# A down projection by seven products of quarters instead of eight, in a fused transformer layer on one core

## The chip, the cores and the metric

The kernel runs on one core of a Trainium2 chip. That core has five engines, each with a queue of its own that is worked off in order: TensorE (PE, products; PEld is its loading of the stationary operand), VectorE (DVE), ScalarE (ACT), GpSimd (POOL) and SyncE (SP, which here only issues transfers). They meet through semaphores. Products are written to banks of PSUM; all other tiles (named `block` in the profile) lie in SBUF. The metric is the device time of one execution in microseconds.

## The reference

One layer of a diffusion backbone on 512 latent tokens of width 1024, with 256 context tokens: attention and a state-space branch side by side, an output projection, and then a gated MLP. All in float32. What bears on the change is the end of it:

```python
def conv_glu(h, w_up, conv_w, conv_b, w_down):
    gate, val = jnp.split(h @ w_up, 2, axis=-1)
    gate = depthwise_conv(gate, conv_w, conv_b)
    return (jax.nn.gelu(gate, approximate=False) * val) @ w_down
...
        ffn_x = conv_glu(modulate(rms_norm(x, ffn_pre_norm[l]), mod_x[3], mod_x[4]),
                         w_up[l], ffn_conv_w[l], ffn_conv_b[l], w_down[l])
        x = x + mod_x[5] * rms_norm(ffn_x, ffn_post_norm[l])
```

The hidden width is 2816, so the down projection (`w_down`) is a product of 512 x 2816 by 2816 x 1024. Its rows are then normalised, multiplied by a row vector and added to x.

## The kernel before

Each float32 operand of a large product is split in two parts, `hi` (ScalarE copies the value into a shorter format, line 497) and `lo` (VectorE subtracts, line 498), and each product is done as three: hi x hi, hi x lo, lo x hi. So every operand costs a ScalarE copy and a VectorE subtraction, and every tile of a product three TensorE instructions.

The work runs in this order: modulation vectors and the input projections, the state-space branch beside the attention, the output projection (`natural_gemm`, products in line 1289), the up projection of the MLP (22 pairs of column blocks; products in line 751), the gating (`gated`, lines 1412 to 1423, one column block of 128 hidden units at a time, kept in `gT` with the hidden unit on the partition), and the down projection (lines 1469 to 1501). That last one runs over two halves of 512 output columns. For each half it takes the 22 hidden blocks in turn: the left operand (`gT[k]`, split once and kept for the second half), the right one (a 128x512 piece of the weights, loaded and split each time), and 4 tiles of 128 tokens x 3 products (line 1476). After the last blocks of a tile its squares are summed (line 1496), it is multiplied by the row `g2` (line 1497), and once both halves are there `last` normalises, adds and stores it (lines 1455 to 1467).

Three row vectors are computed as columns by `modfinish` (from line 1264). To become a row on all partitions a column is written to memory word by word (line 1276) and read back as one row for all 128 partitions (line 1278); both transfers are issued by GpSimd (`G`).

The order in which each engine does its work is set neither by the program text nor at run time. `plan` first traces the program, then places it by a list scheduler with prices for each kind of instruction, and at the same time gives each tile a place in the working memory of `UNITS` units of 1 KB per partition. What comes out is a fixed order on each engine. A tile whose place is taken waits until the former user has finished.

## Time and profile before

| what | value |
| --- | --- |
| median of 3 runs | 1001.02 us (999.69 to 1004.33) |
| span of the profiled execution, first to last instruction | 994.4 us |
| what lies around it, against the median of the runs | 6.6 us |
| last output-projection products end | about 619 us |
| last up-projection products end | 877.9 us |
| last down-projection products end | 986 us |

The profiled execution has no time of its own beside its span; the table sets the span against the median. The page of the profile lists the busy time of each engine, the chain of work that ended last, and groups of instructions by line with their mean duration. A line such as L498 is that of a helper, called from many places. "xN" is a count, "<-" after an idle time names what ended it. Shapes are partitions x elements.

### The profile page before, as it was taken

The page shows a single profiled execution, that of the slowest core. Times are in us where ns is not written, and L with a number is a line of the kernel's source. Part 1 is how long each engine was busy: PE and PEld are TensorE (multiplying, and loading weights), DVE is VectorE, ACT ScalarE, POOL GpSimd, SP SyncE. Part 2 cuts the span into 40 slices and gives each one's busy share as a digit, 9 for nine tenths or more (in the row PEclk, how much of TensorE's full clock was granted, in tenths as well). Part 3 has the DMA queues.
Part 4 walks back from the last instruction along what each step waited for, and adds up shares of the span by engine and source line. Part 5 has one row for each costly group of instructions (what it writes and reads, how often), then busy time and mean ns, then how long its engine had stood idle before and what let it go on. Part 6 is the DMA issues. An engine that isn't in the chain of part 4 may idle for free.

```text
span 994.4 us, 14412 instructions
## 1 busy us (share of the span) xinstructions
PE 971.8 (98%) x5224; PEld 825.9 (83%) x5224; DVE 700.9 (70%) x1304; ACT 501.4 (50%) x994; POOL 259.5 (26%) x223
## 2 busy tenths in 40 slices
PE   9999999999998999999999999999999999999996
PEld 8888888888876888888888888888888888888885
DVE  5999866988896989978789997952515442773406
ACT  4545337568566787687787324842314323452101
POOL 0001001765697886656541000000000000000000
PEclk7999999999998999999999999999999999999999
DMA  9922101012222242331566965431223221354422
GB/s 350 362 74 85 53 1 44 22 48 81 67 57 54 56 111 78 99 74 46 153 259 230 323 160 199 148 127 64 106 85 106 106 85 43 110 177 137 158 76 84
DMA packets 42214, 116.88 MB, mean 118 GB/s; under 512 B 5776, under 2 KB 8736, under 8 KB 42144
## 3 DMA queue, kind: packets, MB, share of 16 engines
q1 hardware_dynamic: 41440, 114.30, 34.8%
q0 software_dynamic: 528, 1.59, 0.5%
q8 instruction: 41, 0.67, 0.3%
q14 instruction: 29, 0.24, 0.1%
q10 hardware_dynamic: 176, 0.09, 0.0%
HBM read 96.02 MB, written 4.21 MB: 101 GB/s over the span
## 4 chain that ended last, share of the span: by engine, by line
PE 49%; DVE 6%; DMA 4%; issue 2%; ACT 1%; SPq 0%; POOL 0%; DVEq 0%; ACTq 0%; POOLq 0%
PE banks L751 26%; PE banks L1476 12%; PE banks L1175 4%; PE banks L1205 3%; PE banks L1193 2%; DVE block L498 2%; DMA block<-block 1%; DMA mod_rows<-mod 1%; DVE block L586 1%; PE banks L1109 1%; DMA block<-mod_rows 1%; ACT block L1179 1%; DVE smalls L1177 1%; DMA block<-in_wmod_dram 0%; DVE smalls L524 0%
## 5 line engine op out<-in xcount | busy, mean ns | idle before, releaser
L751 PE MATMUL banks<-block,block 128*128 128x512 f32 (+1 forms) x2132 | 448.3, 360 | 1.7 <-DVE block L1385 1.1
L751 PEld LDWEIGHTS banks<-block,block 128*128 128x128 f32 x2132 | 358.8, 188 | 62.5 <-issue 1.6
L498 DVE TENSOR_TENSOR block<-block,block 128x512 fp32r<-128x512 f32 (+5 forms) x252 | 227.0, 923 | 125.7 <-PE banks L751 47.8
L497 ACT ACTIVATE block<-block 128x512 fp32r<-128x512 f32 (+5 forms) x252 | 181.4, 743 | 207.8 <-PE banks L751 48.1
L1476 PE MATMUL banks<-block,block 128*128 128x512 f32 x496 | 116.6, 389 | 0.0
L1182 POOL TENSOR_TENSOR block<-block,smalls 128x768 f32<-128x768 f32 x64 | 97.3, 1527 | 60.7 <-DVE smalls L1181 38.4
L1476 PEld LDWEIGHTS banks<-block,block 128*128 128x128 f32 x496 | 93.0, 188 | 19.5
L1175 PE MATMUL banks<-block,block 128*128 128x512 f32 (+1 forms) x384 | 95.1, 357 | 1.4 <-DMA block<-block 0.7
L1276 POOL DMA_DIRECT2D mod_rows<-mod x3 | 2.9, 975 | 351.4 <-DVE mod L1272 351.4
L498 DVE TENSOR_TENSOR block<-banks,block 128x256 fp32r<-128x256 f32 (+1 forms) x156 | 83.2, 555 | 14.7 <-ACT block L497 12.9
L497 ACT ACTIVATE block<-banks 128x256 fp32r<-128x256 f32 (+1 forms) x156 | 73.0, 498 | 32.4 <-PE banks L1193 17.7
L1289 PE MATMUL banks<-block,block 128*128 128x512 f32 x384 | 88.6, 390 | 0.0
L1289 PEld LDWEIGHTS banks<-block,block 128*128 128x128 f32 x384 | 71.8, 188 | 14.5
L1193 PE MATMUL banks<-cst,block 128*128 128x128 f32 x384 | 66.9, 279 | 4.1 <-DVE block L498 3.7
L1205 PE MATMUL banks<-block,block 128*128 128x256 f32 x384 | 68.7, 299 | 0.8 <-DVE block L498 0.8
L1175 PEld LDWEIGHTS banks<-block,block 128*128 128x128 f32 x384 | 59.6, 190 | 10.2 <-ACT block L1179 2.7
L586 DVE SCALAR_TENSOR_TENSOR block<-block,block 128x1024 f32<-128x1024 f32 x52 | 62.6, 1219 | 4.1 <-DMA block<-in_wmod_dram 1.9
L1177 DVE TENSOR_REDUCE smalls<-banks 128x1 f32<-128x768 f32 x64 | 60.8, 950 | 6.6 <-PE banks L1175 5.9
L1179 ACT ACTIVATE block<-banks,smalls 128x768 f32<-128x768 f32 x64 | 57.7, 902 | 13.2 <-DVE smalls L1177 7.6
L786 DVE SCALAR_TENSOR_TENSOR block<-banks,cwh,block 128x510 f32<-128x510 f32 (+3 forms) x88 | 51.1, 620 | 14.4 <-ACT block L782 13.9
L1205 PEld LDWEIGHTS banks<-block,block 128*128 128x128 f32 x384 | 55.9, 191 | 5.3 <-DVE block L498 1.1
L1193 PEld LDWEIGHTS banks<-cst,block 128*128 128x128 f32 x384 | 47.7, 143 | 14.1 <-DVE block L498 3.9
(216 smaller groups left out, 1064.1 us busy)
## 6 DMA issues: line engine op xcount, KB each, us to landing
block<-in_wmod_dram SPq DMA_DIRECT2D x48, 512.0 KB, 6.9
block<-in_wup_dram SPq DMA_DIRECT2D x44, 512.0 KB, 3.8
block<-in_wdn_dram SPq DMA_DIRECT2D x44, 256.0 KB, 2.8
block<-block SPq DMA_DIRECT2D x32, 256.0 KB, 3.0
block<-in_wout_dram SPq DMA_DIRECT2D x16, 512.0 KB, 5.9
block<-block SPq DMA_DIRECT2D x56, 128.0 KB, 2.3
block<-in_wxbc_dram SPq DMA_DIRECT2D x12, 512.0 KB, 3.4
block<-in_wz_dram SPq DMA_DIRECT2D x16, 256.0 KB, 7.1
```

The costliest lines, as they stand in the source:

```text
L497: act(hi, src, AF.Copy)
L498: (lo_eng or V).tensor_tensor(out=lo, in0=src, in1=hi, op=ALU.subtract)
L586: V.scalar_tensor_tensor(out=junk, in0=wt, scalar=0.5, in1=vec, op0=ALU.mult, op1=ALU.mult, accum_out=acc)
L751: mm(po, lhsT=wf(k, pt[0]), rhs=xf(k, pt[1]), start=(k == 0 and pt == parts[0]), stop=(k == nk - 1 and pt == parts[-1]))
L1175: mm(sc[:, o : o + n], lhsT=q_[:, x_, qi * P : (qi + 1) * P], rhs=kk[:, y_, :], start=part == 0, stop=part == 2)
L1177: V.reduce_max(nm, sc[:, :T], axis=AX.X, negate=True)
L1179: act(pe, sc[:, :T], AF.Exp, bias=nm, scale=1.0, accum_out=sm_)
L1182: G.tensor_tensor(out=pe, in0=pe, in1=sm_.to_broadcast([P, T]), op=ALU.mult)
L1193: nc.tensor.transpose((tx if c < NX else tc_)[:, o : o + P], pe[:, s_ : s_ + P], ident)
L1205: mm(po[:, half * 256 : half * 256 + 256], lhsT=vst(c), rhs=rhs, start=(part == 0 and c == 0), stop=(part == 1 and c == NKT - 1))
L1289: mm(po[i][:, nh * 512 : nh * 512 + 512], lhsT=l[lp][:, i * P : (i + 1) * P], rhs=w[wp][:, nh * 512 : nh * 512 + 512], start=(k == 0 and l ...
L1476: mm(po[i], lhsT=l[lp][:, i * P : (i + 1) * P], rhs=w[wp], start=(k == 0 and lp == 0 and wp == 0), stop=(k == NF - 1 and lp == 1))
```

## The change

The down projection is now written as a product of 2 x 2 quarters: the tokens in two halves of 256, the hidden blocks in even and odd ones, the output columns in two halves of 512. Eight products of quarters would be needed in the plain way. Here seven are made, of sums and differences of quarters (the Winograd form of Strassen's scheme), and their results are combined.

- Left operands: for each pair of hidden blocks GpSimd computes four mixtures S1 to S4 of 128x256 (`mixed`, in `gated`). With A11, A12 and A22 from `gT` itself there are seven left operands; each is split when its sweep comes to it (so 7 x 11 splits of 128x256).
- Right operands: B11, B21, B22 are loaded; T1 to T4 are differences of loaded quarters, made on VectorE (`right_of`, line 1514 of the new kernel), T2 and T4 in the place of the former difference, T3 in the place of a loaded quarter. Each right operand is split too (7 x 11 splits of 128x512). 99 pieces of weights are loaded instead of 44.
- A `sweep` runs over the 11 pairs, with 2 tiles of 128 tokens x 3 products each (line 1521). Buffers are rotated: 6 for loaded pieces (`raws`), 8 for left operands (`ls`), 7 for right ones (`ws_`).
- The sweeps are, in the order of the program: S1 T1, S2 T2, A22 T4, S3 T3, A11 B11, S4 B22, A12 B21. The fourth, sixth and seventh go on adding to a bank of an earlier one. Copies of banks on ScalarE (line 1549) and sums on VectorE (lines 1555, 1572, 1574) give the four quarters of the output, and six of the eight multiplications by `g2` go to GpSimd (line 1482).
- `UNITS` is 212 instead of 200; a scratch area for transfers issued by GpSimd is made smaller in return.
- Both transfers of `modfinish` are issued by ScalarE.

```diff
-UNITS, EDGE, MARGIN = 200, 168, 2500
+UNITS, EDGE, MARGIN = 212, 168, 2500
...
         with nc.allow_non_contiguous_dma(reason="a column to a row"):
-            G.dma_start(out=scratch[n].rearrange("j p -> p j"), in_=ms)
+            nc.scalar.dma_start(out=scratch[n].rearrange("j p -> p j"), in_=ms)
         row = t4()
-        G.dma_start(out=row, in_=scratch[n : n + 1].rearrange("o j p -> o (j p)").to_broadcast([P, D]))
+        nc.scalar.dma_start(out=row, in_=scratch[n : n + 1].rearrange("o j p -> o (j p)").to_broadcast([P, D]))
...
         gT.append(cv)
+        if j % 2:
+            ga, gb = gT[-2:]
+            m = t4(P, 4, 256)
+            G.tensor_tensor(out=m[:, 0], in0=ga[:, late], in1=gb[:, late], op=ALU.add)
+            G.tensor_tensor(out=m[:, 1], in0=m[:, 0], in1=ga[:, early], op=ALU.subtract)
+            G.tensor_tensor(out=m[:, 2], in0=ga[:, early], in1=ga[:, late], op=ALU.subtract)
+            G.tensor_tensor(out=m[:, 3], in0=gb[:, early], in1=m[:, 1], op=ALU.subtract)
+            mixed.append([m[:, i] for i in range(4)])
...
+    def right_of(name, q):
+        if name[0] == "B":
+            return quarter(q, int(name[1]) - 1, int(name[2]) - 1)
+        x = quarter(q, *{"T1": (0, 1), "T2": (1, 1), "T3": (1, 1), "T4": (1, 0)}[name])
+        if name in ("T1", "T3"):
+            y = quarter(q, 0, 0 if name == "T1" else 1)
+            t = right[q] = t2() if name == "T1" else x
+        else:
+            t = y = right[q]
+        V.tensor_tensor(out=t, in0=x, in1=y, op=ALU.subtract)
+        return t
+
+    def sweep(po, lname, rname, first=False, done=None):
+
+        def products(i, q, l, w):
+            for n, (lp, wp) in enumerate(((0, 0), (0, 1), (1, 0))):
+                mm(po[i], lhsT=l[:, lp, i * P : (i + 1) * P], rhs=w[wp], start=first and q == 0 and n == 0,
+                   stop=q == PAIRS[-1] and n == 2, skip_group_check=not first)
 
         tail = []
...
+        for q in PAIRS:
+            l = nextof(ls)
+            split(l[:, 0, :], l[:, 1, :], left_of(lname, q))
+            ww = nextof(ws_)
+            w = ww[:, 0, :], ww[:, 1, :]
+            split(*w, right_of(rname, q))
+            if q in PAIRS[:-3]:
+                for i in range(2):
+                    products(i, q, l, w)
             else:
-                tail.append((k, w, lefts[k]))
+                tail.append((q, l, w))
...
+    sweep(W, "S1", "T1", first=True, done=kept(p5))
+    sweep(X, "S2", "T2", first=True, done=kept(p6))
+    sweep(Y, "A22", "T4", first=True)
...
+    sweep(X, "S3", "T3", done=after_p7)
...
+    sweep(Z, "A11", "B11", first=True, done=after_p1)
...
+    sweep(W, "S4", "B22", done=after_p3)
...
+    sweep(Z, "A12", "B21", done=after_p2)
...
-    nc = bacc.Bacc("TRN2", target_bir_lowering=False, num_devices=1)
+    nc = bacc.Bacc("TRN2", target_bir_lowering=False, num_devices=1, dynamic_dma_scratch_size=4096)
```

What the planner makes of it is seen in the order of each engine. A row names the line, the operation, the tile written, then the tiles read and the shape; `block_a_b` is the b-th tile, in a place of its own.

First VectorE in the down projection. Before, splits of weights follow one another:

```order
L498 TENSOR_TENSOR block_1213_7822<-block_1064_7171,block_1056_7057 128x512
L498 TENSOR_TENSOR block_1213_7822<-block_1064_7171,block_1203_7756 128x512
L498 TENSOR_TENSOR block_989_6546<-block_1092_7420,block_1056_7057 128x512
L498 TENSOR_TENSOR block_1062_7120<-block_1064_7171,block_1213_7822 128x512
L498 TENSOR_TENSOR block_971_6414<-block_1092_7420,block_1062_7120 128x512
```

In the changed kernel, in the stretch of the third and fourth sweep, there are three kinds (L1514 the differences of weights, L498 with 128x512 the right splits, with 128x256 the left ones):

```order
L1514 TENSOR_TENSOR block_1135_7543<-block_1018_6728,block_1135_7543 128x512
L1514 TENSOR_TENSOR block_1137_7570<-block_1018_6728,block_1137_7570 128x512
L498 TENSOR_TENSOR block_1126_7457<-block_1131_7489,block_1126_7457 128x512
L498 TENSOR_TENSOR block_1024_6737<-block_979_6453,block_1024_6737 128x256
L498 TENSOR_TENSOR block_865_5474<-block_1133_7516,block_865_5474 128x512
L498 TENSOR_TENSOR block_975_6398<-block_998_6588,block_975_6398 128x256
L1514 TENSOR_TENSOR block_1110_7456<-block_1110_7456 128x512
L1514 TENSOR_TENSOR block_1137_7570<-block_1108_7455,block_1137_7570 128x512
L1514 TENSOR_TENSOR block_1139_7585<-block_1108_7455,block_1139_7585 128x512
L498 TENSOR_TENSOR block_1076_7194<-block_1133_7516,block_1076_7194 128x512
```

Each step of the new sweeps has a left and a right split of its own, and in the first four a difference ahead of them, where before a step had at most one left and one right split.

Second, the transfers of the column-to-row step, in the output projection. Before, they stood on GpSimd, with nothing between them:

```order
L1276 DMA mod_rows<-mod 128x8x1
L1278 DMA block_769_5109<-mod_rows 128x1024
L1276 DMA mod_rows<-mod 128x8x1
L1278 DMA block_787_5183<-mod_rows 128x1024
L1357 TENSOR_TENSOR block_916_5755<-block_916_5755,block_769_5109 128x512
```

Now they stand on ScalarE, among copies of weights (L497) and sums of squares of the output projection's tiles (L1341):

```order
L1276 DMA mod_rows<-mod 128x8x1
L497 ACTIVATE block_883_5525<-block_624_4015 128x1024
L497 ACTIVATE block_888_5533<-block_733_4770 128x1024
L1278 DMA block_795_5180<-mod_rows 128x1024
L1276 DMA mod_rows<-mod 128x8x1
L1341 ACTIVATE block_771_5100,smalls<-banks 128x1024
L1341 ACTIVATE block_771_5100,smalls<-block_707_4588 128x1024
L497 ACTIVATE block_926_5810<-block_797_5183 128x1024
L1278 DMA block_786_5144<-mod_rows 128x1024
L497 ACTIVATE block_923_5805<-block_580_3726 128x1024
L497 ACTIVATE block_929_5863<-block_576_3712 128x1024
L1341 ACTIVATE block_703_4580,smalls<-banks 128x1024
```

A row transfer waits for the column transfer ahead of it to land, and what stands behind it waits with it.

Third, VectorE at the very end. Before, the last tile's chain (L524 and L528 are steps of the reciprocal root) runs straight to its own scale-and-add:

```order
L524 SCALAR_TENSOR_TENSOR smalls<-smalls 128x1
L528 SCALAR_TENSOR_TENSOR smalls<-smalls 128x1
L524 SCALAR_TENSOR_TENSOR smalls<-smalls 128x1
L528 SCALAR_TENSOR_TENSOR smalls<-smalls 128x1
L1466 SCALAR_TENSOR_TENSOR block_986_6541<-block_986_6541,smalls,block_968_6408 128x512 x2
```

Now (the same line is L1475) other tiles' scale-and-adds stand in that chain:

```order
L528 SCALAR_TENSOR_TENSOR smalls<-smalls 128x1 x2
L1475 SCALAR_TENSOR_TENSOR block_1104_7451<-block_1104_7451,smalls,block_1103_7446 128x512
L524 SCALAR_TENSOR_TENSOR smalls<-smalls 128x1
L528 SCALAR_TENSOR_TENSOR smalls<-smalls 128x1
L1475 SCALAR_TENSOR_TENSOR block_1106_7453<-block_1106_7453,smalls,block_1133_7516 128x512
L524 SCALAR_TENSOR_TENSOR smalls<-smalls 128x1
L1475 SCALAR_TENSOR_TENSOR block_1107_7454<-block_1107_7454,smalls,block_1131_7489 128x512
L528 SCALAR_TENSOR_TENSOR smalls<-smalls 128x1
L1475 SCALAR_TENSOR_TENSOR block_1104_7451<-block_1104_7451,smalls,block_1103_7446 128x512
L1475 SCALAR_TENSOR_TENSOR block_1105_7452<-block_1105_7452,smalls,block_1088_7318 128x512 x2
```

Four operations of 128x512 on three other tiles come between the last tile's steps and its own two.

80 lines of the change are left out of this document (55 added, 25 removed).

## The prediction

> **What bounds the kernel now.** I read the page's head and clock first, then the chain of waits in order of time, then the busy time by stretches.
>
> ```profile
> span 994.4 us, 14412 instructions
> PE 971.8 (98%) x5224; PEld 825.9 (83%) x5224; DVE 700.9 (70%) x1304; ACT 501.4 (50%) x994; POOL 259.5 (26%) x223
> PEclk7999999999998999999999999999999999999999
> 631.97 220.07 PE banks L751 x1076
> ...
> 877.88 108.21 PE banks L1476 x477
> 986.17 0.70 ACT block L1496 x2
> ...
> 990.82 0.66 DVEq L1570
> ```
>
> TensorE is busy 98% at nearly full clock. A busy PE alone proves little, but the chain does: from 632 us to the end of the products at 986 it consists almost only of PE, and it ends with a short run of ScalarE and VectorE work. So each product less in the down projection (L1476) is its own time less, as long as its operands come in time. One product costs 108.21 / 477 = 0.2269 us. The stretches say who has room to feed it (columns: length, then busy us and count of PE, PEld, DVE, ACT, POOL, then clock, DMA share, GB/s):
>
> ```profile
> 280.00:300.00 20.00, 17.33 (x91) 12.94 (x89) 18.71 (x31) 14.01 (x30) 19.33 (x17) 1.00 0.25 60
> 300.00:350.00 50.00, 45.69 (x277) 39.50 (x277) 39.34 (x67) 35.64 (x91) 40.39 (x35) 0.93 0.24 63
> 750.00:800.00 50.00, 50.00 (x223) 41.40 (x222) 27.29 (x31) 20.39 (x25) 0.00 (x0) 1.00 0.31 107
> 852.00:878.00 26.00, 26.00 (x117) 21.53 (x116) 19.03 (x32) 14.56 (x26) 0.00 (x0) 1.00 0.44 154
> 900.00:932.00 32.00, 32.00 (x143) 26.50 (x142) 13.88 (x24) 6.73 (x11) 0.00 (x0) 1.00 0.59 206
> 986.00:994.40 8.40, 0.75 (x4) 0.29 (x2) 4.45 (x15) 1.37 (x4) 0.00 (x0) 0.84 0.33 125
> ```
>
> In the up and down projections DVE is about half busy and GpSimd idle. TensorE's own gaps lie elsewhere: 7.0 us between 280 and 350, 7.65 us in the last 8.4.
>
> **Products.** Before, the down projection is 22 x 4 x 2 x 3 = 528 products of 128x512; now 7 sweeps x 11 pairs x 2 tiles x 3 = 462. That is 66 x 0.2269 = **15.0 us** less on the path. A step (one pair, two tiles) is 6 products, 1.361 us. By the order, 480 products stood behind the last one of the up projection, and now 441 do, 100.1 us; 21 products, 3.5 steps, are ahead of it.
>
> **VectorE, the feeder.** This is what is paid for it:
>
> ```profile
> 850.79 6.10 DVE L498 TENSOR_TENSOR block<-block,block 128x512 fp32r<-128x512 f32 x10
> L498 DVE TENSOR_TENSOR block<-block,block 128x512 fp32r<-128x512 f32 x31 | 20.8, 689 | 38.6 <-PE banks L1476 24.6 <-issue 8.7 <-ACT block L497 5.2
> L498 DVE TENSOR_TENSOR block<-banks,block 128x256 fp32r<-128x256 f32 x74 | 30.3, 413 | 3.2 <-ACT block L497 2.2
> L1497 DVE TENSOR_TENSOR block<-banks,block 128x512 f32<-128x512 f32 x8 | 5.5, 686 | 23.8 <-ACT block L1496 23.8
> L498 DVE TENSOR_TENSOR block<-block,block 128x512 fp32r<-128x512 f32 x150 | 116.2, 795 | 74.7 <-PE banks L1476 26.9 <-PE banks L751 18.9 <-issue 17.3
> L1163 POOL TENSOR_TENSOR block<-block,block 128x256 fp32r<-128x256 f32 x24 | 20.6, 865 | 4.4 <-ACT block L1162 4.3
> ```
>
> Ten 128x512 operations in a row took 6.10 us: (6.10 - 0.69) / 9 = 0.602 us each, 0.09 less than one alone. So a 128x256 one takes 0.413 - 0.09, about 0.33 us. Before, 66 operands of 128x512 were split (22 left, 44 right). Now there are 77 right operands at 0.602, 77 left ones at 0.33 and 44 differences of weights at 0.602, together 46.4 + 25.4 + 26.5 = 98.3 us against 39.7. The order puts 19 differences and 10 right splits ahead of the last gating product of the up projection. Up to there DVE was half busy, so this part is hidden. Behind it, up to the last split, come 67 right and 67 left splits, 25 differences and 11 operations on finished banks (0.60 each, by L1497's row): 40.3 + 22.1 + 15.1 + 6.6 = 84 us beside 100.1 us of PE. As a whole DVE keeps up.
>
> Not everywhere, though. There are 7 buffers of right operands, so split n waits for the products of step n - 7, plus ScalarE's copy. Split 17 can thus end at about 6.5 x 1.361 + 1.0 + 0.6 = 10.4 us behind the last up product, and is needed at 12.5 x 1.361 = 17.0: a lead of 6.6 us, and no more. From there to split 43 all 25 differences fall: 26 x 0.602 + 30 x 0.33 + 25 x 0.602 = 40.6 us of DVE for 26 steps of PE, 35.4 us. The lead shrinks by 5.2, to **1.4 us**. After split 43, 34 right and 30 left splits and the 11 operations are 37 us for 34 steps, 46.3 us, and the lead comes back.
>
> So the question is what else falls into that stretch. GpSimd mixes the left operands, 44 operations of 128x256, 44 x 0.865 = 38 us, where it was idle; that is hidden, but the order leaves eight of them behind the last gating product. Where GpSimd works, a DVE operation on two blocks is longer: 795 ns over the whole kernel, 689 in the stretch without GpSimd (the rows of x150 and x31). Eight of them cost DVE between 8 x 0.106 = 0.8 us (the mean lengthening) and 8 x 0.865 = 6.9 us (DVE stands still through each). The Trainium skill (SBUF — State Buffer, "Who interferes with whom") speaks against this edit: a DVE instruction with two SBUF inputs and a GpSimd instruction that reads SBUF exclude each other for the whole instruction. By it the upper figure stands; the two means agree that there is a cost, and none of these rows shows its size for one pair.
>
> **Loads.** Now 99 weight quarters instead of 44:
>
> ```profile
> block<-in_wdn_dram SPq DMA_DIRECT2D x44, 256.0 KB, 2.8
> GB/s 350 362 74 85 53 1 44 22 48 81 67 57 54 56 111 78 99 74 46 153 259 230 323 160 199 148 127 64 106 85 106 106 85 43 110 177 137 158 76 84
> 869.08 2.72 ACT L497 ACTIVATE block<-block 128x512 fp32r<-128x512 f32 x5 [2.45 <-PE banks L1476]
> L497 ACT ACTIVATE block<-banks 128x256 fp32r<-128x256 f32 x74 | 28.2, 386 | 5.2 <-PE banks L1193 2.8 <-PE banks L751 1.7 <-DVE smalls L1181 0.2
> ```
>
> 99 x 262,144 bytes at the best slice's 362 GB/s are 72 us, fine for the whole. The fourth sweep (T3) takes 22 of them. One of its six buffers is held through landing (2.8), difference (0.69), ScalarE's copy (0.63), split (0.69) and some 0.6 of handovers: 5.4 us for three steps, 1.8 each against 1.361. Over 11 steps that is up to 4.8 us late; nothing if they were loaded ahead. ScalarE does 77 x (0.52 + 0.28) = 62 us of copies, 6 bank copies and 8 squares, under 75 in all: hidden.
>
> **The stall** therefore lies between 0 (0.8 us against the 1.4 of lead) and 6.9 + 4.8 - 1.4 = 10.3 us. I take **+4**, under the middle, since the x31 row shows a mean lengthening nearer to the lower end.
>
> **ScalarE issues the transfers.**
>
> ```profile
> 569.81 1.08 POOL L1276 DMA_DIRECT2D mod_rows<-mod  x1 [39.54 <-DVE mod L1272]
> 581.68 0.57 POOL L1278 DMA_DIRECT2D block<-mod_rows  x1 [10.79 <-DMA mod_rows<-mod]
> 584.46 0.90 POOL L1276 DMA_DIRECT2D mod_rows<-mod  x1 [2.21 <-DVE mod L1272]
> 595.09 0.56 POOL L1278 DMA_DIRECT2D block<-mod_rows  x1 [9.73 <-DMA mod_rows<-mod]
> mod_rows<-mod POOLq DMA_DIRECT2D x3, 4.0 KB, 10.3
> 534.71 84.27 PE L1289 MATMUL banks<-block,block 128*128 128x512 f32 x371
> 595.72 0.18 ACT L1341 ACTIVATION_READ_ACCUMULATOR block<-block 128x1 f32 x1
> 601.10 1.03 ACT L1341 ACTIVATE block<-banks 128x1024 f32<-128x1024 f32 x1 [1.92 <-PE banks L1289]
> block<-in_cv_dram ACTq DMA_DIRECT2D x1, 8.0 KB, 3.1
> ```
>
> On GpSimd the wait of some 10 us for the first transfer held up nobody. On ScalarE it holds up whatever is queued: the order has two weight copies between the first pair, then the squares of the output projection's first tile and a copy ahead of the second row transfer, and behind that more weight copies and the second tile's squares. PE meanwhile runs products from 534.7 to 619. If the transfers take as long as before, ScalarE is free again at about 595.7, and the second tile's squares start at 601.1: 5.4 us of room. I take **0** (down to -1.6, TensorE's idle between 620 and 632 by the same stretches; upward see the rival). The third row is read back behind a landing long past.
>
> ```profile
> 620.00:632.00 12.00, 10.44 (x83) 9.70 (x82) 11.86 (x48) 10.95 (x30) 1.78 (x1) 1.00 0.51 177
> 990.07 1.41 DVE L1466 SCALAR_TENSOR_TENSOR block<-block,smalls,block 128x512 f32<-128x512 f32 x2
> out_dram<-block SPq DMA_DIRECT2D x8, 256.0 KB, 2.1
> ```
>
> **The end.** From the last product to the end it takes 8.2 us (986.17 to 994.4). Now the scale-and-add of rows finished two sweeps ago stands in the last tile's chain: four more L1466-like operations at 0.66 us. Between 0 (they fit its gaps) and +2.6; I take **+1.5**. **More memory** makes the whole program a different order. What that gives is not in the diff: nothing in the middle, 3.5 us gained (half of the 7.0 between 280 and 350) or as much lost; **0**.
>
> Sum: 994.4 - 15.0 + 4 + 1.5 = 984.9 us of span. The median of the runs, 1001.02, stands 6.6 above the profiled span, so **991.5 us**.
>
> **Rivals.** (A) The forecast, chance 0.60. (B) No stall, no longer end, and the new order closes half of the gaps at 280 to 350: 994.4 - 15.0 - 3.5 + 6.6 = 982.5. For it: DVE has 84 us of work in 100; against: a lead of 1.4 us. 0.17. (C) VectorE becomes the bound in the sweeps with differences, with GpSimd's lock and the late loads at their full price: 994.4 - 15.0 + 10.3 + 2.6 + 6.6 = 998.9, no difference that can be told. For it: 40.6 us of work against 35.4; against: the lead and the mean lengthening of 0.106. 0.16. (D) Slower: ScalarE stands in its two waits. Both landings are in series, so each microsecond more than 10.3 costs two, less the 5.4 of room. At 24 us each it is 2 x 13.7 - 5.4 = 22 us of late squares, normalisation and transposes, 991.5 + 22 = 1013.5. It turns the change into a loss from about 17.8 us on (2 x 7.5 - 5.4 = 9.6, all of the gain). For it: 1024 single words on a queue on which no row shows such a pattern; against: ScalarE's own queue landed 8 KB in 3.1 us. 0.07.
>
> **How the numbers follow.** What can be told from no change here is about 0.5%, 996 to 1006. Faster: A but 0.05, B, 0.05 of C: 0.77. The same: 0.05 of A, 0.10 of C, 0.01 of D: 0.16. Slower: 0.07. The range goes from below B to beyond C, 981 to 1001; outside lie most of D and the tails.
>
> **What would show it.** Right: 462 products at 0.227 us, PE without gaps up to its last up product, gaps of some 4 us in all within the second to fourth sweep, ended by DVE's splits or by a load of the weights; no gap of PE near 590 to 620. B: no gaps in the sweeps. C: 10 us of them, and DVE operations near 0.8 us beside GpSimd. D: ScalarE idle behind the row transfers and PE idle at the transposes. The forecast is wrong if a gap opens elsewhere than in the sweeps, or if the new order moves the first 860 us by more than 4.

## The result, and the profile after

The changed kernel takes 995.18 us (median of 13 runs, 989.83 to 1001.82), the kernel before, timed beside it, 1002.35 us (13 runs, 997.74 to 1007.40). The ratio is 0.9936, 95% interval 0.9907 to 0.9964: faster by 0.64%. The forecast was 991.5 us, 3.7 us less.

The two profiled executions, however, are equally long: spans of 994.4 and 994.3 us. A timed run is 1.7 to 2.4 us longer than its own span, 1.8 in most. By that the profiled execution before would be a run of some 996.2 us, an estimate, 6 below the median of 1002.35; that of the changed kernel is a run of 996.11 us, 0.9 above its median. So the two profiles show where time is won and lost, but not the 7.2 us between the medians. The head of the page and the clock row of the kernel after:

```profile
span 994.3 us, 14782 instructions
PE 959.9 (97%) x5158; PEld 814.2 (82%) x5158; DVE 778.1 (78%) x1442; ACT 541.8 (54%) x1088; POOL 299.7 (30%) x267
PEclk7999999999999999999999999899999999999998
L1521 PE MATMUL banks<-block,block 128*128 128x512 f32 x462 | 109.6, 392 | 3.4 <-ACT block L497 1.7 <-DVE block L498 1.6
```

TensorE is busy 11.9 us less, and idle 11.8 us more (34.4 us against 22.6). The stretches show where. For the kernel after, and in the second fence for the one before, with columns as in the prediction (length, then busy us and count of PE, PEld, DVE, ACT, POOL, then clock, DMA share, GB/s):

```profile
619.00:635.00 16.00, 9.87 (x67) 9.27 (x66) 13.94 (x55) 11.66 (x34) 1.26 (x1) 0.79 0.37 126
900.00:932.00 32.00, 29.38 (x125) 22.49 (x124) 30.09 (x61) 20.16 (x44) 0.00 (x0) 1.00 0.65 206
932.00:960.00 28.00, 27.27 (x118) 21.71 (x119) 25.66 (x50) 21.88 (x46) 1.86 (x1) 1.00 0.77 243
982.80:994.30 11.50, 0.00 (x0) 0.00 (x0) 7.70 (x26) 0.69 (x2) 0.00 (x0) 0.72 0.48 183
```

```profile
619.00:635.00 16.00, 14.44 (x116) 13.67 (x115) 15.67 (x64) 14.94 (x44) 1.78 (x1) 1.00 0.39 133
```

Three places lose time. In the sweeps TensorE is idle for 2.62 + 0.73 = 3.35 us (1.37 in the third sweep, 1.25 in the fourth, 0.73 at the start of the fifth), where it had no gap before. From the last product to the end it takes 11.5 us instead of 7.7. And at the transposes between output and up projection it is idle for 6.1 us instead of 1.6, and its granted clock there is 0.79 instead of 1.00. The rows of TensorE and VectorE at the transposes of the kernel after (start, length, engine, line, operation, and in brackets the idle time before with what ended it):

```profile
603.63 1.28 DVE L1373 SCALAR_TENSOR_TENSOR block<-block,smalls,block 128x1024 f32<-128x1024 f32 x1 [3.65 <-DMA block<-mod_rows]
617.41 1.91 PE L1381 MATMUL banks<-cst,block 128*128 128x128 f32 x16
622.47 0.89 PE L751 MATMUL banks<-block,block 128*128 128x256 f32 x3 [3.15 <-ACT block L1384]
626.34 4.87 PE L751 MATMUL banks<-block,block 128*128 128x256 f32 x27 [2.98 <-DVE block L1385]
```

The chain of waits shows the other two places: weights that land late (two pieces for the differences T3 of the fourth sweep, then one of the fifth, which goes to ScalarE's copy without a difference), then 41.83 us of products without a gap (183 of them, 0.2286 us each), and behind the last product a chain of small VectorE steps.

```profile
920.80 3.93 DMA block<-in_wdn_dram
...
926.08 4.37 DMA block<-in_wdn_dram
...
933.06 5.14 DMA block<-in_wdn_dram
938.22 0.64 ACT block L497
938.90 41.83 PE banks L1521 x183
980.76 0.70 ACT block L1481 x2
...
989.21 0.66 DVEq L1658
989.87 0.66 DVE block L1475
```

### The profile page after: what moved, and what is told of

It reads as the page before. It is cut to its first block, busy times and chain, and to the rows that moved or that the text cites. A ratio compares the mean times of both kernels' runs of the same rounds, so it can differ in the third digit from the quotient of the medians.

```text
span 994.3 us, 14782 instructions
## 1 busy us (share of the span) xinstructions
PE 959.9 (97%) x5158; PEld 814.2 (82%) x5158; DVE 778.1 (78%) x1442; ACT 541.8 (54%) x1088; POOL 299.7 (30%) x267
## 5 line engine op out<-in xcount | busy, mean ns | idle before, releaser
L751 PE MATMUL banks<-block,block 128*128 128x512 f32 (+1 forms) x2132 | 454.4, 363 | 7.4 <-ACT block L1384 3.1
L497 ACT ACTIVATE block<-block 128x512 fp32r<-128x512 f32 (+5 forms) x340 | 217.4, 665 | 207.1 <-PE banks L751 47.5
L498 DVE TENSOR_TENSOR block<-block,block 128x512 fp32r<-128x512 f32 (+4 forms) x340 | 269.0, 825 | 65.8 <-ACT block L497 35.1
L1521 PE MATMUL banks<-block,block 128*128 128x512 f32 x462 | 109.6, 392 | 3.4 <-ACT block L497 1.7
L1175 PE MATMUL banks<-block,block 128*128 128x512 f32 (+1 forms) x384 | 95.7, 357 | 1.4 <-DMA block<-block 1.1
L498 DVE TENSOR_TENSOR block<-banks,block 128x256 fp32r<-128x256 f32 (+1 forms) x156 | 83.5, 557 | 10.9 <-ACT block L497 6.9
L1289 PE MATMUL banks<-block,block 128*128 128x512 f32 x384 | 89.3, 391 | 0.0
L497 ACT ACTIVATE block<-banks 128x256 fp32r<-128x256 f32 (+1 forms) x156 | 74.4, 497 | 19.8 <-PE banks L1193 12.2
L1289 PEld LDWEIGHTS banks<-block,block 128*128 128x128 f32 x384 | 71.8, 188 | 14.9 <-DVE block L1230 0.4
L1179 ACT ACTIVATE block<-banks,smalls 128x768 f32<-128x768 f32 x64 | 57.8, 903 | 12.3 <-DVE smalls L1177 11.6
L1430 POOL TENSOR_TENSOR block<-block 128x256 f32<-128x256 f32 x11 | 10.3, 949 | 171.6 <-DVE block L1422 93.8
L786 DVE SCALAR_TENSOR_TENSOR block<-banks,cwh,block 128x510 f32<-128x510 f32 (+3 forms) x88 | 51.3, 621 | 10.7 <-ACT block L782 10.0
```

Source lines behind the costliest of these rows:

```text
L497: act(hi, src, AF.Copy)
L498: (lo_eng or V).tensor_tensor(out=lo, in0=src, in1=hi, op=ALU.subtract)
L751: mm(po, lhsT=wf(k, pt[0]), rhs=xf(k, pt[1]), start=(k == 0 and pt == parts[0]), stop=(k == nk - 1 and pt == parts[-1]))
L1175: mm(sc[:, o : o + n], lhsT=q_[:, x_, qi * P : (qi + 1) * P], rhs=kk[:, y_, :], start=part == 0, stop=part == 2)
L1179: act(pe, sc[:, :T], AF.Exp, bias=nm, scale=1.0, accum_out=sm_)
L1289: mm(po[i][:, nh * 512 : nh * 512 + 512], lhsT=l[lp][:, i * P : (i + 1) * P], rhs=w[wp][:, nh * 512 : nh * 512 + 512], start=(k == 0 and l ...
```

## How the executions are compared

Each kernel below differs from another by a line or two, but the planner then orders the whole program anew. So times alone don't tell what an edit did. For each profiled execution I took TensorE's records and added up its idle time (length less busy time, as in the rows above) in four stretches: up to the last product of the output projection, the 16 us behind it (the transposes), from there to the last product, and the end. The granted clock is 1 or 0.5 in the records; half of TensorE's busy time at 0.5 is put down as lost to the clock (an upper bound; 3.3 to 6.8 us of it are the first 50 us of the program, 13.7 in before_212_gpsimd and 13.5 in no_differences). What is left of the span is the work at full clock. Ratios are against the kernel before on the same chip, with 95% intervals.

| kernel | ratio | idle up to the transposes | at the transposes | up and down projection | end | lost to the clock | work at full clock |
| --- | --- | --- | --- | --- | --- | --- | --- |
| before | 1 | 13.4 | 1.6 | 0.0 | 7.7 | 8.4 | 963.5 |
| before_scalar_rows | 1.0135 (1.0104 to 1.0165) | 18.6 | 10.1 | 0.7 | 7.9 | 14.9 | 961.4 |
| before_212_scalar | 0.9932 (0.9909 to 0.9954) | 11.9 | 4.5 | 0.0 | 7.7 | 9.8 | 958.7 |
| before_212_gpsimd | 0.9940 (0.9917 to 0.9962) | 15.4 | 0.3 | 0.0 | 7.6 | 13.7 | 959.7 |
| after | 0.9936 (0.9907 to 0.9964) | 13.4 | 6.1 | 3.4 | 11.6 | 12.1 | 947.8 |
| no_differences | 0.9890 (0.9850 to 0.9930) | 13.2 | 9.0 | 0.0 | 11.0 | 16.8 | 941.9 |
| gpsimd_rows | 0.9867 (0.9835 to 0.9898) | 11.4 | 4.0 | 2.5 | 11.5 | 11.5 | 946.9 |
| after_words_15000 | 0.9887 (0.9865 to 0.9909) | 15.1 | 2.9 | 0.5 | 10.3 | 10.2 | 947.5 |
| gpsimd_words_15000 | 0.9921 (0.9903 to 0.9940) | 20.2 | 2.5 | 0.8 | 11.9 | 8.7 | 945.5 |
| gpsimd_rows_tail | 0.9829 (0.9810 to 0.9848) | 11.1 | 2.6 | 0.6 | 12.3 | 5.0 | 946.9 |
| gpsimd_rows_urgent | 0.9902 (0.9870 to 0.9934) | 11.4 | 6.2 | 5.6 | 9.7 | 10.7 | 946.2 |
| gpsimd_rows_urgent_v | 0.9863 (0.9827 to 0.9899) | 12.7 | 3.3 | 4.2 | 9.7 | 6.8 | 948.4 |
| words_15000_urgent | 0.9850 (0.9818 to 0.9881) | 14.1 | 3.7 | 5.1 | 9.6 | 9.6 | 944.5 |
| gpsimd_rows_208 | 0.9817 (0.9784 to 0.9849) | 15.1 | 3.9 | 2.0 | 10.3 | 6.2 | 946.4 |

The last column carries the products. The four kernels with eight products have 958.7 to 963.5, mean 960.8; the nine complete ones with seven have 944.5 to 948.4, mean 946.7. The difference is 14.1 us, and 15.7 between the two kernels of the case. The two groups do not overlap, and the 15.0 us of the forecast are there, within the spread of the orders (4.8 us in the first group, 3.9 in the second). All else stands in the columns of idle time and clock. (The names say what differs: who issues the row transfers, scalar or gpsimd; 208 or 212 units; the rest comes below.)

## The experiments

### One part undone, one part alone

My first theory was that the transfers issued by ScalarE make the gap at the transposes. Its rival was the new order that 212 units give. The first run takes ScalarE's transfers back:

```diff
-            nc.scalar.dma_start(out=scratch[n].rearrange("j p -> p j"), in_=ms)
+            G.dma_start(out=scratch[n].rearrange("j p -> p j"), in_=ms)
-        nc.scalar.dma_start(out=row, in_=scratch[n : n + 1]...)
+        G.dma_start(out=row, in_=scratch[n : n + 1]...)
```

> The changed kernel with the column-to-row transfers issued by GpSimd again; products, memory and the rest as changed. Theory (the transfers on ScalarE cost the transposes): TensorE's idle time between 617 and 632 us falls from the 5.4 us of the changed kernel towards the 1.6 of the kernel before, the first copies of the transposes (L1384) start near 619.8 instead of 621.8, and the time is 3 to 4 us lower, ratio near 0.990. Rival (the new order that 212 units give is the cause, whoever issues): the gap stays at 4 to 6 us and the ratio at 0.9935. Second rival (the granted clock there, 0.72 in the one execution, is chance): the gap differs by execution, with no relation to the issuer.

Measured: 986.52 us, ratio 0.9867, so 0.7% better than the changed kernel, more than the theory asked for. But the gap is still 4.0 us, and behind it stand 10.2 us at half clock instead of 6.8, so the transposes explain 2 us of it at most.

The second run puts ScalarE's transfers alone into the kernel before (the same two lines, the other way).

> The kernel before with one part of the change alone: ScalarE issues the column-to-row transfers; 200 units, eight products. Theory (the transfers on ScalarE cost the transposes): TensorE is idle for 4 to 6 us between 617 and 634 us instead of 1.6, and the time is 3 to 4 us longer, ratio near 1.004. Rival (the order that 212 units give is the cause): idle 1.6 there, ratio 1.000 within its interval.

Measured: 1014.41 us, ratio 1.0135, three times the loss expected. Here the transfers are late in earnest. The issues on ScalarE's queue, ScalarE and VectorE behind them, and the transposes:

```profile
577.48 5.56 ACTq L1276 DMA_DIRECT2D mod_rows<-mod  x2
587.71 2.02 ACTq L1278 DMA_DIRECT2D block<-mod_rows  x1
608.77 0.34 ACTq L1278 DMA_DIRECT2D block<-mod_rows  x1
609.21 1.06 ACT L497 ACTIVATE block<-block 128x1024 fp32r<-128x1024 f32 x1 [12.59 <-DMA mod_rows<-mod]
609.89 1.22 DVE L1354 TENSOR_TENSOR block<-banks,block 128x1024 f32<-128x1024 f32 x1 [19.92 <-DMA block<-mod_rows]
625.86 3.25 PE L1381 MATMUL banks<-cst,block 128*128 128x128 f32 x15 [3.26 <-DVE smalls L1343]
634.29 1.19 PE L751 MATMUL banks<-block,block 128*128 128x256 f32 x4 [5.18 <-DVE smalls L528]
```

```profile
DMA to landing us min/median/max: 10.2/10.4/26.1
DMA to landing us min/median/max: 3.9/7.7/22.1
```

The second fence gives the time from issue to landing of the column's transfer (first line) and of the row's (second line), three each. The second column and the first row were in flight together, and with them loads of the up weights, x and others; they took 26.1 and 22.1 us, and VectorE stood still for 19.9 us, ScalarE for 12.6. TensorE then lacked 10.1 us of work at the transposes.

The third run has everything of the change but the seven products (212 units, the smaller scratch area, ScalarE's transfers), and a later one 212 units and the smaller scratch area alone.

```diff
-UNITS, EDGE, MARGIN = 200, 168, 2500
+UNITS, EDGE, MARGIN = 212, 168, 2500
-    nc = bacc.Bacc("TRN2", target_bir_lowering=False, num_devices=1)
+    nc = bacc.Bacc("TRN2", target_bir_lowering=False, num_devices=1, dynamic_dma_scratch_size=4096)
```

> The kernel before with all of the change but the seven products: 212 units, the smaller descriptor memory and ScalarE's transfers. It tells what the products' scheme alone brings. Theory: ratio near 1.004, by the transposes alone, so that the scheme itself brings about 10 us (15.0 less 3.4 in the sweeps and 3 at the end, give or take 1). Rival (the new order of the first 620 us takes or gives): the time differs by more than 4 us from the run with ScalarE's transfers alone, and TensorE's idle time before 617 us is not the 13.3 us of the kernel before.

> The kernel before with 212 units and the smaller descriptor memory alone: eight products, transfers issued by GpSimd. With it stand four kernels of 212 units, with eight or seven products and with either issuer: ScalarE 993.9 and 995.2, GpSimd (this one) and 986.5. First theory (the seven products bring what their terms say, 15.0 less 3.4 in the sweeps and 3.9 at the end, so 7 to 8 us, and ScalarE's pair happens to differ in the first 620 us): 994, ratio 0.993. Second theory (the issuer costs 9 to 13 us whatever the products, so that at 212 units the scheme brings nothing): 981 to 985, ratio 0.983.

Measured: 0.9932 with ScalarE's transfers and 0.9940 with GpSimd's. This overturned the theory of a fixed price for ScalarE's issue: 1.35% at 200 units, nothing (0.9932 against 0.9940) at 212 units and eight products, 0.7% at 212 units and seven. It depends on the order in which the transfers happen to stand. And it is the largest surprise of the case: the kernel with all of the change but its products is as fast as the changed kernel (0.9932 and 0.9936). By that pair the seven products bring nothing; by the pair with GpSimd's transfers (0.9940 and 0.9867) they bring 0.7%, the 7 to 8 us of the first theory, but neither pair is clear of the spread that the orders alone give (below). The first expected 994 us for the kernel with 212 units alone and the second 981 to 985; it took 991.74, between the two.

### The stall in the sweeps

The next kernel leaves the differences out: T1 to T4 are single quarters as loaded, so the down projection's result is not the product.

```diff
-        x = quarter(q, *{"T1": (0, 1), "T2": (1, 1), "T3": (1, 1), "T4": (1, 0)}[name])
-        ...
-        V.tensor_tensor(out=t, in0=x, in1=y, op=ALU.subtract)
+        t = quarter(q, *{"T1": (0, 1), "T2": (1, 1), "T3": (1, 1), "T4": (1, 0)}[name])
         return t
```

> The changed kernel without the 44 differences of weight quarters: each of T1 to T4 is one quarter as loaded, so 77 loads instead of 99, and the result of the down projection is not the product. Theory (VectorE's differences and the fourth sweep's loads make the stall): TensorE's 3.4 us of idle time between 877 and 960 us are gone, and the time is 3 to 4 us lower, ratio near 0.990; VectorE is busy 26 us less. Rival (the seven buffers of right operands, or ScalarE's copies, hold the sweeps): gaps of 2 us and more stay, ended by L497, and the ratio stays at 0.9935.

Measured: ratio 0.9890, and no gap in the sweeps:

```profile
900.00:932.00 32.00, 32.00 (x143) 26.50 (x142) 25.25 (x48) 25.83 (x52) 0.00 (x0) 1.00 0.63 194
932.00:960.00 28.00, 28.00 (x125) 23.20 (x124) 25.32 (x46) 22.51 (x48) 3.57 (x2) 1.00 0.83 274
```

From 900 to 932 us VectorE was busy for 30.09 us in the changed kernel; here it is 25.25, and TensorE is busy all the time. Over the whole kernel VectorE is busy 18.6 us less (759.5 against 778.1), not the 26 expected. So in this order the 3.35 us in the sweeps are gone with the differences and their loads; the seven buffers and ScalarE's copies, which are still there, hold nothing up. The work and the loads were not taken apart, and the order has a share too: three kernels below keep the differences and are idle for only 0.5 to 0.8 us.

What ate VectorE's lead in the changed kernel is partly GpSimd. Its last eight mixtures of left operands run from 877.0 to 885.3 us, and VectorE's operations beside them are longer than later ones of the same kind (the last row):

```profile
876.85 1.82 DVE L1514 TENSOR_TENSOR block<-block,block 128x512 f32<-128x512 f32 x2
878.20 1.07 POOL L1429 TENSOR_TENSOR block<-block,block 128x256 f32<-128x256 f32 x1
878.59 1.22 DVE L498 TENSOR_TENSOR block<-block,block 128x512 fp32r<-128x512 f32 x1
901.29 0.68 DVE L498 TENSOR_TENSOR block<-block,block 128x512 fp32r<-128x512 f32 x1
```

Seven differences and splits beside the mixtures take 6.9 us of VectorE's time; at the usual time of each (0.602 and 0.335 us behind 886 us) they would take 3.4. The eight mixtures so cost 3.5 us. Two operations among them that read one operand from a bank (L1422) are not longer, 0.68 and 0.67 us.

The runs of no_differences fall into two groups: three at 984.4 to 987.1 us, with a mean granted clock of 0.985 to 0.990, and three at 993.4 to 993.6 us, all with 0.977. One and the same program differs by 8 us with the clock it is granted.

### The late row

The theory was now: the second row of the modulation lands late, VectorE stands still for it (L1373 or L1354), the four tiles' normalisation is late, TensorE is idle at the transposes, and behind the gap it runs at half clock. The planner expects 5000 ns for a transfer of single words. One number makes it plan for late rows, in the changed kernel and in the one with GpSimd's transfers:

```diff
-DMA_START, DMA_WAIT, DMA_AHEAD, DMA_ALONE, DMA_WORDS = 650, 910, 3000, 0.8, 5000
+DMA_START, DMA_WAIT, DMA_AHEAD, DMA_ALONE, DMA_WORDS = 650, 910, 3000, 0.8, 15000
```

> The changed kernel, with one number of the planner's costs changed: it takes 15000 instead of 5000 ns for a transfer of single words (DMA_WORDS), so that it orders the work for late rows. Nothing computed differs. Theory (the second row of the modulation arrives too late, VectorE stands still for it at L1373 or L1354, the four tiles' normalisation runs late, TensorE is idle at the transposes and then runs for 7 to 14 us at half clock): no wait for mod_rows of over 1 us, TensorE's 6.1 us of idle time at the transposes under 3, and 987 to 991 us, ratio near 0.988. Rival (the row is not what the transposes wait for): the wait is gone, but the idle time stays at 4 to 6 us, and the ratio at 0.9935.

> The same number, 15000 instead of 5000, in the kernel whose transfers GpSimd issues (986.5 us, row waited for 1.6 us, 4.0 us idle at the transposes). Theory of the late row: little is left to gain, 983 to 986. Rival (orders differ by chance): anywhere between 980 and 995, with the idle time before 612 us or the half clock telling the difference.

Measured for the changed kernel: 988.17 us, ratio 0.9887. VectorE no longer waits for the row, and the stretch behind the output projection reads

```profile
619.40:635.40 16.00, 13.13 (x103) 11.99 (x101) 15.21 (x58) 14.06 (x35) 1.28 (x1) 1.00 0.69 253
```

with 2.9 us of idle time and full clock. ScalarE's transfers do no harm there. Measured for the other: 991.33 us, ratio 0.9921, worse than the 0.9867 it started from, as its rival allowed: the gap at the transposes is 2.5 us and the clock full, but TensorE is idle for 20.2 us before it instead of 11.4, 17.1 of them between 200 and 509 us. These two agree with the row theory, but other executions do not. In the kernel before VectorE waits longer for the row than in the changed kernel (3.65 us), and TensorE is idle for only 1.6 us at the transposes, at full clock:

```profile
602.35 1.28 DVE L1373 SCALAR_TENSOR_TENSOR block<-block,smalls,block 128x1024 f32<-128x1024 f32 x1 [4.48 <-DMA block<-mod_rows]
```

That wait ends 16.6 us ahead of the last output product, the one in the changed kernel 13.9 us ahead of it. And in gpsimd_rows_urgent (below) VectorE waits for no row, yet the gap is 6.2 us, with half clock behind it. So a late row can make the gap, but it is not the only cause; what else makes it stays open. Nor does it say how long the whole takes.

### What an unchosen order is worth

The kernel with GpSimd's transfers, and 208 units instead of 212:

```diff
-UNITS, EDGE, MARGIN = 212, 168, 2500
+UNITS, EDGE, MARGIN = 208, 168, 2500
```

> The kernel whose transfers GpSimd issues, with 208 units instead of 212: nothing but the places of the buffers and so the planner's order differs. It measures what an order is worth that nobody chose. Theory (an order is worth up to 5 us either way, by idle time ahead of the transposes and half clock behind them): anywhere between 981 and 992 us, the work at full clock within 1.5 us of 946.9. Rival (the order hardly matters, GpSimd's issue is worth its 8.7 us): 986 to 987.5.

Measured: 985.97 us beside 1003.27 us of the kernel before, ratio 0.9817 (0.9784 to 0.9849), the lowest of all, with less memory than its twin of 212 units (0.9867, 0.9835 to 0.9898). The intervals just overlap, and the medians themselves are 985.97 and 986.52 us, the kernel before beside them having taken 1003.27 and 1000.89. So this pair alone does not decide between the theory and its rival. Its work at full clock is 946.4, as expected within 1.5 us. Over the nine complete kernels with seven products the ratio goes from 0.9817 to 0.9936, 1.2%, twice the whole gain of the case. Part of that is the edits, but no edit left the order of the rest of the program as it was. Where memory alone differs (units, and in the first case the scratch area), the difference is 0.6% (0.9940 against 1, eight products) and 0.5% (this pair).

### The end

Behind the last product VectorE works off the last two tiles' normalisation and, among it, four scale-and-adds (L1475) of rows that were complete two sweeps before. The first attempt gives those four to ScalarE and GpSimd, in the kernel with GpSimd's transfers:

```diff
         for h in (slice(0, 512), slice(512, 1024)):
+            if i >= 2:
+                act(res[i][:, h], res[i][:, h], AF.Copy, scale=c0)
+                G.tensor_tensor(out=res[i][:, h], in0=res[i][:, h], in1=xr[:, h], op=ALU.add)
+            else:
                 V.scalar_tensor_tensor(out=res[i][:, h], ...)
```

> The kernel whose transfers GpSimd issues, with the four scale-and-adds of the rows finished two sweeps ahead done by ScalarE (scale) and GpSimd (add) instead of VectorE. Theory (they stand in the last tile's chain on VectorE and make the end 11.5 us instead of 7.7): the time from the last product to the end falls to 8 to 9 us, and the whole by 2 to 3 us, to 984. Rival (the end is set by the last tile's own chain and by eight stores at once): it stays at 11 us or more, 986.5.

Measured: 982.38 us, ratio 0.9829, by the number what the theory wanted. But not by its reason: the end is 12.3 us, not 8 to 9, and the gain lies elsewhere (4.7 us less lost to the clock at the transposes, 3.5 us less in the first 50 us, 1.9 us less idle time from the transposes to the last product). Its profiled execution is 9.5 us shorter than that of gpsimd_rows, more than the medians differ, so part of these terms is chance of the execution. The rows of GpSimd and VectorE behind the last product say why the end did not shrink:

```profile
966.01 4.93 POOL L1477 TENSOR_TENSOR block<-block,block 128x512 f32<-128x512 f32 x4 [1.56 <-ACT block L1476]
966.31 0.98 DVE L524 SCALAR_TENSOR_TENSOR smalls<-smalls 128x1 f32<-128x1 f32 x1
967.34 1.18 DVE L528 SCALAR_TENSOR_TENSOR smalls<-smalls 128x1 f32<-128x1 f32 x1
969.22 1.73 DVE L524 SCALAR_TENSOR_TENSOR smalls<-smalls 128x1 f32<-128x1 f32 x2
972.21 0.21 DVE L524 SCALAR_TENSOR_TENSOR smalls<-smalls 128x1 f32<-128x1 f32 x1
```

While GpSimd adds, VectorE's steps on a single column take 0.98 (L524) and 1.18 us (L528), and a pair 1.73, where elsewhere they take 0.21, 0.15 and 0.34. Three such encounters cost about 3 us, as much as the four scale-and-adds (0.75 each).

The second attempt leaves them on VectorE, but marks them urgent for the planner; the third, in addition, has VectorE do the last multiplications that GpSimd had.

```diff
+        mark = here()
         last(2 + i, 2)
+        urgent.append(((mark, here()),))
...
-        part_done(i, 1, t12[i], G)
+        part_done(i, 1, t12[i], V)
```

(The last two lines in the third attempt alone.)

> The kernel whose transfers GpSimd issues, with the last steps of the rows finished two sweeps ahead (sum, reciprocal root, four scale-and-adds at L1475) marked urgent for the planner, so that VectorE does them as soon as they are ready, among the splits. Nothing computed differs. Theory (four scale-and-adds and two reciprocal roots of other rows in the last tiles' chain make the end 11.5 us instead of 7.7): the time from the last product to the end falls to 8 to 9 us. Rival (the end is lengthened by GpSimd's multiplications beside VectorE's small steps, 1.0 to 1.2 us each where they meet instead of 0.2): it falls by 1 us at most. The whole: 986.5 less that, give or take 4 for the new order of the rest.

> The same, and the multiplication of rows 0 and 1, right half, by VectorE instead of GpSimd, so that GpSimd is idle at the end. Theory of the four scale-and-adds: no shorter end than with the urgent mark alone, 8 to 9 us. Rival (GpSimd's share of the memory port): the small steps L524 and L528 at 0.2 us throughout, and the end 2 us shorter than with the mark alone.

Measured: 994.35 and 991.11 us. The end falls from 11.5 to 9.75 and 9.65 us, less than the theory asked for and more than its rival, but the sweeps lose more than that. TensorE's rows of the first of them:

```profile
948.46 15.30 PE L1521 MATMUL banks<-block,block 128*128 128x512 f32 x66 [1.27 <-DVE block L498]
966.63 13.46 PE L1521 MATMUL banks<-block,block 128*128 128x512 f32 x58 [2.88 <-DVE block L1574]
```

The urgent steps wait for each other on VectorE in the middle of the sweeps, the sums that must empty a bank (L1574) come late, and the idle time from the up projection to the last product rises from 2.5 to 5.6 and 4.2 us. The ratios are 0.9902 and 0.9863, no better than 0.9867. The four scale-and-adds are so worth about 1.8 us of the end, and nothing once they are paid for elsewhere. Giving GpSimd's two multiplications to VectorE changes nothing (9.75 against 9.65), but tests little: in the second attempt they run from 975.15 to 977.69 us, ahead of the last product (980.09), and meet no small step.

The same mark in the changed kernel planned with 15000 ns:

> The changed kernel (ScalarE issues), planned with 15000 ns for a transfer of single words, and the urgent mark. 988.2 us without the mark, with an end of 10.3 us. Theory: an end of 8 to 9 us and 986 us. If orders differ by chance by 5 us: between 981 and 992, the difference lying ahead of the last product.

Measured: 989.03 us, ratio 0.9850 (0.9818 to 0.9881), against 0.9887 (0.9865 to 0.9909) without the mark; the intervals overlap. The end is 9.6 us instead of 10.3, the sweeps lose 5.1 us instead of 0.5, and there is a gap with half clock at the transposes again.

So 2 us more than before remain even in these kernels (9.6 to 9.75 against 7.7). The traces show what they are. Before, VectorE does one tile's last steps behind the last product: two scale-and-adds (the 1.41 us at 990.07 in the prediction's rows) and three steps L524. In gpsimd_rows_urgent_v, whose last product ends at 975.36 us, it does those of two tiles, four scale-and-adds and six steps L524:

```profile
977.35 0.74 DVE L1475 SCALAR_TENSOR_TENSOR block<-block,smalls,block 128x512 f32<-128x512 f32 x1
979.23 2.07 DVE L1475 SCALAR_TENSOR_TENSOR block<-block,smalls,block 128x512 f32<-128x512 f32 x3
```

From the last product to VectorE's last operation it takes 5.9 us instead of 4.7, and from there to the end, with four stores of these tiles instead of two, 3.7 instead of 3.0. In the changed kernel eight scale-and-adds stand behind the last product, so six more than before (7.8 us, and 3.8 to the end). That the second tile's work can be brought ahead was not tried.

## Why the prediction was right, and where it was wrong

The direction and the range (981 to 1001) held. But the prediction's own sign of being wrong, a gap elsewhere than in the sweeps, appeared too: 6.1 us at the transposes. By its steps:

- **Products, -15.0.** Right: -15.7 in work at full clock between the two kernels of the case, -14.1 between the means of all. That the first is so close to the forecast is partly chance, as kernels with the same products differ by up to 4.8 us.
- **The stall, +4.** Right in size (3.35 us), nearly in place (911 to 939 us, in the third and fourth sweep and at the start of the fifth) and, for this order, in cause: it is gone without the differences, VectorE's work fills the chain from 873.7 to 920.8 us, and then come landings of weights (3.93 and 4.37 us for the fourth sweep, 5.14 for the fifth). The lead of 1.4 us was nearly enough in other orders (0.5, 0.6 and 0.8 us of idle time), so C, with 10 us, was far off.
- **GpSimd beside VectorE.** The prediction left open whether an encounter costs 0.1 us or the whole of GpSimd's instruction, for its eight mixtures 0.8 to 6.9 us. The changed kernel's trace has 3.5 us for them, the middle. A short step of 0.15 to 0.21 us becomes 0.98 to 1.18 beside GpSimd's 1.23 in gpsimd_rows_tail. The Trainium skill (SBUF — State Buffer, "Who interferes with whom"), which has a VectorE instruction with two inputs in SBUF and a GpSimd instruction that reads SBUF wait for each other, agrees with these rows.
- **The end, +1.5 with a bound of 2.6.** Mis-sized: +3.9 (11.6 against 7.7; the prediction's 8.2 for the end before counts from 986.17, but the last product ends at 986.75). The prediction counted the four scale-and-adds, which the urgent mark shows to be worth 1.8 us. The other 2 us were not in the sum: the last steps of a second tile also stand behind the last product, and with them two more stores.
- **ScalarE issues the transfers, 0.** The step looked for one price, and there is none: +13.5 us in the kernel before, nothing at 212 units with eight products, 0.7% or 7 us in the changed kernel against its GpSimd twin, -3 us in the pair planned with 15000 ns (0.9887 against 0.9921). Rival D described the mechanism well (ScalarE standing in the column's wait, with everything behind it waiting), and it did occur, in the kernel before with ScalarE's transfers alone. With the two columns' 10.2 and 26.1 us its formula gives 10.2 + 26.1 - 20.6 - 5.4 = 10.3 us; 13.5 were measured, and the first row's 22.1 us ran beside the second column's landing, not behind it. In the changed kernel's order VectorE had the row 1.3 us later than before (603.63 against 602.35).
- **More memory, a new order, 0 give or take 3.5.** This step failed. "What that gives is not in the diff" was true, but the bound was taken from one place, the gaps between 280 and 350 us, although the whole program is ordered anew. With 212 units and the smaller scratch area alone the kernel before becomes 0.6% faster, the size of the whole result; 208 and 212 units differ by 0.5% (0.9817 and 0.9867, intervals that just overlap).
- **The clock at the transposes, not in the sum.** The profiled execution of the kernel before had full clock there, so the prediction saw idle time of 1.6 us and no more. In the changed kernel 6.1 us of idle time stand there and 1.9 us are lost to the clock behind them. Idle time and clock together are what made 994.3 of the expected 984.9: -15.7 of work, +3.4 in the sweeps, +3.9 at the end, +4.6 at the transposes and before, +3.7 of clock make -0.1. Of the 3.7 us of clock 1.9 stand at the transposes and 1.7 in the first 50 us.
- **The offset of 6.6 us** between the profiled execution before and its median is not what lies around the span. Of it 1.8 us do, in nearly every run that has both numbers. The rest is that the profiled execution was a fast one, with little lost to the clock: its mean granted clock is 0.990, the median of 15 others 0.986. Over 1000 us that is 8 us more at half clock, 4 us lost, an estimate that covers most of the rest. For the changed kernel (994.3 us profiled, 995.18 median) the offset is 0.9 us, and the 5.7 us too much in it hid most of what the sum had missed.

So the number came near in part by luck. The span was missed by 9.4 us (994.3 against 984.9): 2.4 at the end, 4.6 of idle time at the transposes and before them and 3.7 of clock, less 0.7 and 0.7 by which the stall and the products did better (rounded). The offset, 5.7 us too large for the changed kernel, left 3.7 of that. For the direction stand the products: 15 us less against 7.3 us paid in the sweeps and at the end. The other losses in these two executions, 8.3 us, lie at the transposes and ahead of them or in the clock.

That the seven products made the kernel faster is not shown by the pair that differs in them alone with ScalarE's transfers (0.9932 and 0.9936). The pair with GpSimd's (0.9940 and 0.9867) agrees with it, but one pair is within what orders do. What shows it is the work at full clock: 944.5 to 948.4 us in nine kernels against 958.7 to 963.5 in four. The times go the same way: eight of the nine ratios are below all four.

Left open: what makes the gap at the transposes where no row is late; which part of the first 600 us gains by 212 units (the profiled execution of before_212_gpsimd had a bad start, 20.5 and 6.8 us at half clock, and is 6.7 us above the median of that kernel); and how the kernel would do with the changed down projection behind an unchanged order of the first 620 us, which no run could hold fixed.

## What to carry to other kernels

Where a planner orders the whole program, compare an edit with the spread that orders alone give (here 0.5 and 0.6% where memory alone differs, 1.2% over all kernels with the same products), and separate work at full clock, idle time and clock, stage by stage, before a gain or a loss is put down to the edit. Where the budget allows, try several orders (a unit of memory more or less, one price in the planner) and keep the best: the best of the nine kernels with seven products stands at 0.9817, the change as first planned at 0.9936. Work moved to an idle engine or to an earlier place is paid for where it lands.

## What was not expected of the hardware

**A gap has a second price.** Behind the output projection the granted clock of TensorE stayed at 1 in all six executions whose longest single gap there was at most 1.8 us, and fell to half, for 6.8 to 17 us, in all eight whose longest gap was 2.0 us or more. Rows of the same 16 us in gpsimd_rows, with a longest gap of 3.09 us, and in gpsimd_rows_tail, with 1.07 us:

```profile
612.30:628.30 16.00, 11.96 (x64) 10.63 (x63) 15.70 (x55) 10.90 (x33) 1.26 (x1) 0.72 0.70 248
```

```profile
609.90:625.90 16.00, 13.40 (x103) 12.11 (x101) 15.50 (x57) 14.64 (x38) 1.69 (x1) 1.00 0.62 228
```

Counted as in the table, the half clock cost 1.9 us in the changed kernel and 2.7 to 6.5 us in the other seven, between a third of the idle time there and a little more than all of it.

The length of a single gap is not shown to be the rule. The idle time in these 16 us separates the same executions as well (at most 3.3 us with full clock, 3.7 or more with half). Elsewhere in these traces single gaps of 2.09 us (gpsimd_words_15000, 347 us), 2.22 (before_212_gpsimd, 509 us) and 2.88 (gpsimd_rows_urgent, 964 us) were followed by full clock, while two gaps of 0.92 and 0.97 us, one behind the other at 332 us in the changed kernel, were followed by 3.4 us of half clock. The Trainium skill (TensorE: Matmul & The Clock Gate, "Part 1: The HAM clock gate") has the clock halved after an idle window of some 3.4 us that runs free of the program; the lengths at half clock here (6.8, 10.2, and 3.4 and 13.7) are multiples of 3.4 us, which agrees, while gaps of 2.0 and of twice 3 us, all shorter than a window, were enough.

**A word-by-word transfer has no fixed landing time.** The same 4 KB column took 8.7 to 15.4 us from issue to landing in nearly all kernels, whichever engine issued it, and 18.1 and 26.1 us in two with ScalarE's transfers. While the one of 26.1 us was in flight (582.7 to 608.8 us), the core's loads ran at up to 412 GB/s; the row of rates, 40 slices of 0.925 us from 575 us on:

```profile
GB/s 270 385 128 2 11 0 62 35 0 31 27 9 13 9 18 44 142 376 412 408 395 412 253 13 22 182 315 191 35 44 22 195 342 293 173 49 31 66 164 319
```

That the loads are the cause was not tested apart.
